# A transformer layer on one core: the compression MLP's first products in fp32 on four column quarters, instead of split in two and summed

## The chip, the cores and the metric

The kernel runs on one core of a Trainium2 chip. The metric is the device time of one execution in microseconds (us); the median of the runs is compared. Five engines work side by side, each through a queue of its own in program order: TensorE (PE, with its weight loads shown apart as PEld), VectorE (DVE), ScalarE (ACT), GpSimd (POOL) and SyncE (SP), which only issues transfers here. They meet at semaphores.

## The reference, cut to what matters

One layer of a causal decoder over 256 tokens of width 1024, in float32: RMSNorm, one input projection `h @ w_in` of 5656 columns, two attention mixers with a gated merge, `w_out`, and a gated convolutional MLP of width 2816. The change is in one small piece of the first mixer, the compression of its keys and values (two groups of 64 features each). Blocks of 32 tokens, 16 apart, are flattened and go through a small MLP; it is called once for keys and once for values:

```python
def compress(kv, pe, w1, w2):                    # kv: (1, 256, 2, 64), w1: (2048, 128)
    b16 = kv.reshape(B, S // 16, 16, G, dh)
    blocks = jnp.concatenate([b16[:, :-1], b16[:, 1:]], axis=2)      # 15 blocks of 32 tokens
    blocks = blocks + pe[None, None, :, None, :]
    flat = blocks.transpose(0, 1, 3, 2, 4).reshape(B, nc, G, 32 * dh)
    return jax.nn.gelu(flat @ w1) @ w2           # flat @ w1: contraction over 2048
```

`flat @ w1` is the piece: for each of the two calls 32 columns (2 groups x 16 places, of which 15 are used), a contraction over 2048 = 16 tiles of 128, and 128 outputs.

## The kernel before, in words

**Units.** All weights come as one stream of 128 x 2048 blocks, one block a unit, in a list `units` that one loop walks. A unit `u` is loaded by SP into a tile `u.raw` (pool `wraw`, three buffers of tag `raw`), split into two fp32r tiles by `hi_of` (ACT copies `raw` to `u.hi`, L127) and `lo_of` (DVE subtracts, `u.lo = raw - hi`, L131), multiplied on PE by `u.mm`, and the result in PSUM is written out by `u.evac`. Activations are split the same way (`hTh`, `hTl`), so that a product in full precision is three fp32r products: hi x hi and lo x hi (L180), hi x lo (L185), 48 matmuls of 256 moving columns for a usual unit. The tiles `hi` and `lo` have three buffers each too.

**Order.** The order on every engine is the order of the code in the loop; there is no scheduler. In step `i` of the loop: `load_to(i + 5)` issues loads up to unit `i + 4`; then the small work of attention; `lo_of(i + 1)`; `u.mm(u)` for unit `i`; `hi_of(i + 2)`; and `u.evac`. SP waits with a load until the buffer of `raw` that it goes to has been read.

**The stretch around the change.** Units 0 and 1 are multiplied first and together; unit 0 gives the raw keys and values for compression. `ev_cmp` scales them, adds the position term and writes a tile `f` of 128 x 4 x 256 (keys: parts 0 and 1, values: parts 2 and 3; a part has 32 columns `c` by 8 tiles `m`, with `m` running fastest). Unit 2 is a wider one. Units 3 and 4 are queries (`qa`). Units 5, 7 and 9 are queries of the second mixer (`qb`, evacuated on DVE by `ev_qb`, L448). **Units 6 and 8 are the weights `w1` of the compression**, for keys and for values. From unit 10 on come keys, values and gates of the second mixer, and from step 9 on the attention items run between the units' products.

**The compression before.** `split_cmp` splits `f` into `XC`, in which hi and lo columns stand side by side (L331 on ACT, L332 on DVE); `w1_hi` and `w1_lo` split units 6 and 8 on ACT (L404) and DVE (L409), hi and lo side by side as well. `mm_w1` (L419) then needs 16 matmuls for each of the two: 64 stationary columns (hi and lo of the activations), 256 moving columns (hi and lo of the weights), which fill a 64 x 256 corner of PSUM (`ph`). `cmp_sum`, `cmp_fold` add the parts up: S2 is built by ACT (L732) and DVE (L733), its lower half zeroed by POOL, and two small matmuls with the 0/1 matrix `E2` fold it (L740). `gates_of` (L429, L430) and `q_parts` (`QS`, L441 on ACT and L442 on DVE) are unrelated work that stands in DVE's queue between.

## Time and profile before

| | before |
|---|---|
| time, median of 3 runs | 396.79 us (402.17, 396.23, 396.79) |
| the profiled execution: own time | 396.06 us |
| its span in the trace | 394.3 us |
| PE busy | 387.1 us (98%), 3404 instructions |
| DVE busy | 292.5 us (74%) |
| ACT busy | 224.7 us (57%) |
| POOL busy | 32.0 us (8%) |
| granted clock of TensorE in the span | 0.998 |

Own time and span differ by 1.8 us, which lie outside the trace. PE's busy time counts overlapping records once; a record's duration is longer than the distance to the next record, since matmuls are pipelined, so that the pace is read from starts. An fp32 matmul shows as two records, an fp32r matmul as one.

### The profile page before, as it was taken

The page shows a single profiled execution, that of the slowest core. Times are in us where ns is not written, and L with a number is a line of the kernel's source. Part 1 is how long each engine was busy: PE and PEld are TensorE (multiplying, and loading weights), DVE is VectorE, ACT ScalarE, POOL GpSimd, SP SyncE. Part 2 cuts the span into 40 slices and gives each one's busy share as a digit, 9 for nine tenths or more (in the row PEclk, how much of TensorE's full clock was granted, in tenths as well). Part 3 has the DMA queues.
Part 4 walks back from the last instruction along what each step waited for, and adds up shares of the span by engine and source line. Part 5 has one row for each costly group of instructions (what it writes and reads, how often), then busy time and mean ns, then how long its engine had stood idle before and what let it go on. Part 6 is the DMA issues. An engine that isn't in the chain of part 4 may idle for free.

```text
span 394.3 us, 8025 instructions
## 1 busy us (share of the span) xinstructions
PE 387.1 (98%) x3404; PEld 381.1 (97%) x3404; DVE 292.5 (74%) x486; ACT 224.7 (57%) x316; POOL 32.0 (8%) x62
## 2 busy tenths in 40 slices
PE   8999999999999999999999999999999999999993
PEld 7999999999999999999999999999999999999993
DVE  5989899994877776468887599676594774947764
ACT  5987755774974665654644766545265452653513
POOL 7110000001000000250333000000000000000001
PEclk9999999999999999999999999999999999999999
DMA  7966673345233345452538246662734727347102
GB/s 275 418 252 257 244 264 134 126 175 235 108 109 114 117 170 183 167 182 111 199 153 288 86 170 240 233 235 103 304 128 194 251 104 287 135 185 263 59 0 106
DMA packets 11555, 72.60 MB, mean 184 GB/s; under 512 B 1280, under 2 KB 1664, under 8 KB 3584
## 3 DMA queue, kind: packets, MB, share of 16 engines
q1 hardware_dynamic: 11088, 71.25, 48.7%
q10 hardware_dynamic: 432, 0.85, 0.6%
q8 instruction: 26, 0.43, 0.4%
q14 instruction: 9, 0.07, 0.0%
HBM read 71.05 MB, written 1.05 MB: 183 GB/s over the span
## 4 chain that ended last, share of the span: by engine, by line
PE 92%; ACT 2%; DVE 2%; DMA 2%; issue 0%; POOL 0%; SPq 0%; POOLq 0%; ACTq 0%
PE ps_d L180 26%; PE ps_d L185 13%; PE ps_o L180 13%; PE ps_s L624 8%; PE ps_t L624 7%; PE ps_o L185 6%; PE ps_d L284 3%; PE ps_d L346 2%; PE ps_t L180 2%; DMA first<-in_first_dram 2%; PE ps_o L904 1%; PE ps_o L540 1%; PE ps_t L891 1%; PE ps_o L1028 1%; PE ps_s L180 1%; PE ps_d L419 1%
## 5 line engine op out<-in xcount | busy, mean ns | idle before, releaser
L131 DVE TENSOR_TENSOR wlo<-raw,whi 128x2048 fp32r<-128x2048 f32 (+2 forms) x62 | 134.7, 2175 | 0.9 <-ACT whi L127 0.7
L127 ACT ACTIVATE whi<-raw 128x2048 fp32r<-128x2048 f32 (+2 forms) x62 | 115.1, 1858 | 31.2 <-DMA raw<-in_wts_dram 27.2
L180 PE MATMUL ps_d<-hTh,whi 128*128 128x256 f32 x384 | 90.2, 280 | 0.0
L180 PE MATMUL ps_d<-hTl,whi 128*128 128x256 f32 x384 | 89.2, 278 | 0.0
L180 PEld LDWEIGHTS ps_d<-hTh,whi 128*128 128x128 f32 x384 | 72.2, 188 | 0.7 <-issue 0.5
L180 PEld LDWEIGHTS ps_d<-hTl,whi 128*128 128x128 f32 x384 | 72.3, 188 | 0.0
L185 PE MATMUL ps_d<-hTh,wlo 128*128 128x256 f32 x384 | 48.0, 278 | 0.0
L185 PEld LDWEIGHTS ps_d<-hTh,wlo 128*128 128x128 f32 x384 | 45.7, 188 | 0.1
L180 PE MATMUL ps_o<-hTh,whi 128*128 128x256 f32 x160 | 36.9, 277 | 0.0
L180 PE MATMUL ps_o<-hTl,whi 128*128 128x256 f32 x160 | 36.8, 277 | 0.0
L579 ACT ACTIVATE C<-U,small 128x256 f32<-128x256 f32 x22 | 12.0, 594 | 43.3 <-DVE U L575 43.3
L180 PEld LDWEIGHTS ps_o<-hTl,whi 128*128 128x128 f32 x160 | 30.1, 188 | 0.0
L180 PEld LDWEIGHTS ps_o<-hTh,whi 128*128 128x128 f32 x160 | 30.0, 188 | 0.0
L583 DVE SCALAR_TENSOR_TENSOR C<-U,small,C 128x256 f32<-128x256 f32 x44 | 19.4, 482 | 7.5 <-ACT C L579 7.4
L575 DVE TENSOR_TENSOR U<-ps_d,R 128x512 f32<-128x512 f32 x6 | 4.1, 691 | 22.1 <-PE ps_d L185 18.3
L185 PE MATMUL ps_o<-hTh,wlo 128*128 128x256 f32 x160 | 19.8, 276 | 0.0
L185 PEld LDWEIGHTS ps_o<-hTh,wlo 128*128 128x128 f32 x160 | 18.9, 188 | 0.0
L868 ACT ACTIVATE E<-E,ast 128x256 f32<-128x256 f32 (+1 forms) x32 | 14.2, 451 | 8.0 <-DVE ast L863 7.9
L575 DVE TENSOR_TENSOR U<-ps_o,R 128x512 f32<-128x512 f32 x5 | 3.4, 689 | 16.7 <-PE ps_o L185 16.7
L1254 POOL TENSOR_TENSOR tiny<-cst,tiny 128x1 f32<-128x1 f32 x2 | 0.4, 190 | 168.8 <-ACT sq L1253 168.8
L131 POOL TENSOR_TENSOR wlo<-raw,whi 128x1024 fp32r<-128x1024 f32 x3 | 7.7, 2573 | 74.1 <-ACT whi L127 74.1
L624 PE MATMUL ps_s<-whi,al 128*128 128x256 f32 x88 | 12.1, 276 | 0.0
(287 smaller groups left out, 768.7 us busy)
## 6 DMA issues: line engine op xcount, KB each, us to landing
raw<-in_wts_dram SPq DMA_DIRECT2D x61, 1024.0 KB, 4.8
first<-in_first_dram SPq DMA_DIRECT2D x7, 384.0 KB, 7.1
raw<-in_wts_dram SPq DMA_DIRECT2D x2, 560.0 KB, 9.0
xn<-in_xn_dram SPq DMA_DIRECT2D x2, 512.0 KB, 9.0
xT<-in_xT_dram SPq DMA_DIRECT2D x1, 1024.0 KB, 6.8
gf<-in_g_final_dram ACTq DMA_DIRECT2D x1, 512.0 KB, 3.6
out_dram<-Y SPq DMA_DIRECT2D x1, 512.0 KB, 2.6
out_dram<-Y SPq DMA_DIRECT2D x1, 320.0 KB, 2.4
```

What stands on the lines that cost most here:

```text
L127: A.activation(u.hi[:, u.o + c0:u.o + c1], u.raw[:, c0:c1], AF.Copy)
L131: (eng or V).tensor_sub(u.lo[:, u.o + c0:u.o + c1], u.raw[:, c0:c1], u.hi.bitcast(F32)[:, u.o + c0:u.o + c1])
L180: T.matmul(po, l, r, start=start and bank not in banks, stop=False, skip_group_check=True)
L185: T.matmul(po, l, r, start=False, stop=stop and n == len(ks) - 1, skip_group_check=True)
L284: T.matmul(u.p[:, i], l[:, kt, i * 128:i * 128 + 128], r[:, kt], start=kt == 0 and i == 0 and q == 0, stop=kt == 7 and q == 2, skip_group_ ...
L346: T.matmul(u.p[:, i], l[:, kt, i * 128:i * 128 + 128], r[:, kt], start=kt == 0 and i == 0 and q == 0, stop=kt == 7 and q == 2, skip_group_ ...
L419: T.matmul(p[0:64, i].rearrange("p h c -> p (h c)"), x, w[:, m % 8], start=m == 0, stop=m == 15, skip_group_check=True)
L575: V.tensor_tensor(out=U[:, :, 2:], in0=u.p, in1=bc(rt["R2"], 2), op=OP.mult)
L579: A.activation(C[:, c], U[:, c, 2:], AF.Identity, scale=CW(2, t), bias=CB[:, t:t + 1])
L583: V.scalar_tensor_tensor(C[:, c], U[:, c, w:w + S], CW(w, t), C[:, c], op0=OP.mult, op1=OP.add)
L624: T.matmul(ffn["y"][t][ch][:, b:e] if own is None else own, x[:, kt, t * 128:t * 128 + 128], w[:, kt, ch * 512 + b:ch * 512 + e], start=st ...
L868: A.activation(self.E[:, i], self.E[:, i], AF.Exp, bias=mn[:, i:i + 1], scale=-1.0, accum_out=dn[:, i:i + 1])
```

## The change

The compression's first products are made in fp32, without hi and lo. `f` itself is the stationary operand (32 columns for the first eight tiles of the contraction, 31 for the others, which start one block later), read in steps of eight elements, and the raw weights are the moving operand (128 columns). The 16 tiles of the contraction are dealt out to four column quarters of the array: tile `m` writes PSUM partitions 32 (m mod 4) and up, so that four sums stand below each other. The products of keys and values stand together, at step 8; step 6 has no product of its own. `E2` now adds up the four quarters, S2 is one ACT copy of 128 x 256.

The weights of units 6 and 8 no longer go through `raw`: they are loaded in two halves each to tiles of their own, `w1k` (tag MA, free after the first units) and `w1v` (two of the three buffers of tag PT, free until the attention needs them), and neither is split. `f` moves to tag MB. `lo_of(7)` now stands in step 5, behind `hi_of(7)`, instead of in step 6.

```diff
--- before.py
+++ after.py
@@ -85,8 +85,8 @@
 
 
 class Unit:
-    def __init__(self, n, mm, evac=None, split=None, pre=None, o=0):
-        self.n, self.mm, self.evac, self.split, self.pre, self.o = n, mm, evac, split, pre, o
+    def __init__(self, n, mm, evac=None, load=None, pre=None, o=0):
+        self.n, self.mm, self.evac, self.load, self.pre, self.o = n, mm, evac, load, pre, o
         self.raw = self.hi = self.lo = None
 
 
@@ -136,8 +136,10 @@
 
     def hi_of(i):
         if 2 <= i < len(units):
+            if units[i].load is not None:
+                return
             split_tiles(units[i])
-            (units[i].split or (split_hi, split_lo))[0](units[i])
+            split_hi(units[i])
 
     def lo_of(i):
         if 2 <= i < len(units):
@@ -152,13 +154,17 @@
                 split_lo(units[i], 0, 1024)
                 split_lo(units[i], 1024, 2048)
                 return
-            (units[i].split or (split_hi, split_lo))[1](units[i])
-
-    def load_range(u, c0, c1, q=None):
-        (q or nc.sync).dma_start(u.raw[:, c0:c1], bass.AP(tensor=a["wts"].tensor, offset=a["wts"].offset + u.off + c0,
+            if units[i].load is None:
+                split_lo(units[i])
+
+    def load_range(u, c0, c1, q=None, dst=None):
+        (q or nc.sync).dma_start(u.raw[:, c0:c1] if dst is None else dst, bass.AP(tensor=a["wts"].tensor, offset=a["wts"].offset + u.off + c0,
                                                           ap=[[u.n, 128], [1, c1 - c0]]))
 
     def load_unit(u):
+        if u.load is not None:
+            load_w1(u.load)(u)
+            return
         u.raw = wraw.tile([128, UW], F32, name="raw", tag="raw")
         load_range(u, 0, u.n)
 
@@ -304,14 +310,10 @@
 
     xr = {}
 
-    def xc_tile():
-        xr["XC"] = att.tile([128, 4, 8, 65], F32R, name="XC", tag="MB")
-        V.memset(xr["XC"].bitcast(F32)[:, :, :, 64], 0.0)
-
     def ev_cmp(u):
         R = rt["R"]
         t = att.tile([128, 2, 2, 128], F32, name="E", tag="E", bufs=2)
-        f = att.tile([128, 4, 256], F32, name="PT", tag="PT", bufs=3)
+        f = att.tile([128, 4, 256], F32, name="XC", tag="MB")
         p = u.p.rearrange("p i (s two) -> p two i s", two=2)
         Rv = R.rearrange("p (s two) -> p two s", two=2)
         for g in range(2):
@@ -326,11 +328,6 @@
                                 in1=pv[:, hf, i, None, :].to_broadcast([128, 32, 8]), op=OP.add)
         xr["f"] = f
 
-    def split_cmp(i):
-        f, XC = xr["f"][:, 2 * i:2 * i + 2].rearrange("p a (c m) -> p a m c", m=8), xr["XC"][:, 2 * i:2 * i + 2]
-        A.activation(XC[:, :, :, 0:32], f, AF.Copy)
-        V.tensor_sub(XC[:, :, :, 32:64], f, XC.bitcast(F32)[:, :, :, 0:32])
-
     def mm_first(u):
 
         for v in range(2):
@@ -393,31 +390,27 @@
     units.append(Unit(2048, lambda u: None, ev_ka))
 
 
-    def w1_parts(u, i):
-        dst = (u.hi, u.lo)[i]
-        r = u.raw[:, i * 1024:i * 1024 + 1024].rearrange("p (m c) -> p m c", m=8)
-        return [x[:, :2048].rearrange("p (m h c) -> p m h c", m=8, h=2) for x in (dst, dst.bitcast(F32))] + [r]
-
-    def w1_hi(u):
+    def mm_w1(u):
+        p = rt["ph"] = pd([2, 128])
         for i in range(2):
-            d, _, r = w1_parts(u, i)
-            A.activation(d[:, :, 0], r, AF.Copy)
-
-    def w1_lo(u):
-        for i in range(2):
-            d, h, r = w1_parts(u, i)
-            V.tensor_sub(d[:, :, 1], r, h[:, :, 0])
-
-    def mm_w1(i):
-        def f(u):
-            if i == 0:
-                rt["ph"] = pd([2, 2, 128])
-            p = rt["ph"]
             for m in range(16):
-                w = (u.hi, u.lo)[m // 8][:, :2048].rearrange("p (m c) -> p m c", m=8)
-                x = xr["XC"][:, 2 * i + m // 8, m % 8, m // 8:m // 8 + 64]
-                T.matmul(p[0:64, i].rearrange("p h c -> p (h c)"), x, w[:, m % 8], start=m == 0, stop=m == 15,
+                j, h = m % 4, m // 8
+                x = xr["f"][:, 2 * i + h].rearrange("p (c m) -> p m c", m=8)[:, m % 8, h:32]
+                T.matmul(p[32 * j:32 * j + 32 - h, i], x, xr["w1"][i][m // 8][:, m % 8], start=m < 4, stop=m > 11,
                          skip_group_check=True)
+
+    def load_w1(i):
+        if i == 0:
+            w = att.tile([128, 2, 8, 128], F32, name="w1k", tag="MA")
+            w = [w[:, h] for h in range(2)]
+        else:
+            w = [att.tile([128, 8, 128], F32, name="w1v", tag="PT", bufs=3) for _ in range(2)]
+
+        def f(u):
+            for h in range(2):
+                u.raw = w[h].rearrange("p m c -> p (m c)")
+                load_range(u, 1024 * h, 1024 * h + 1024, dst=u.raw)
+        xr.setdefault("w1", []).append(w)
         return f
 
     def ev_v(u):
@@ -453,7 +446,7 @@
         units.append(Unit(2048, lambda u: mm_plain(u, "t"), ev_k(qa, 2 * i, scale=-0.125)))
     for i in range(3):
         if i:
-            units.append(Unit(2048, mm_w1(i - 1), split=(w1_hi, w1_lo)))
+            units.append(Unit(2048, mm_w1 if i == 2 else lambda u: None, load=i - 1))
         units.append(Unit(2048, mm_plain, ev_qb(2 * i)))
     for i in range(3):
         units.append(Unit(2048, mm_plain, ev_k("kb", 2 * i)))
@@ -727,10 +720,7 @@
     def cmp_sum():
 
         S2 = att.tile([128, 2, 128], F32, name="S2", tag="c1")
-        P.memset(S2[64:128], 0.0)
-        p, s = rt["ph"][0:64], S2[0:64]
-        A.activation(s, p[:, :, 0], AF.Copy)
-        V.tensor_tensor(out=s, in0=p[:, :, 1], in1=s, op=OP.add)
+        A.activation(S2, rt["ph"], AF.Copy)
         cmp_["S2"] = S2
 
     def cmp_fold():
@@ -1083,8 +1073,7 @@
         for up, (g, s) in enumerate(pair):
             P.memset(scB[up * 64:up * 64 + 64, i:i + 1], -0.125 / SLOPE_B[s])
     E2 = att.tile([128, 32], F32, name="E2")
-    P.memset(E2[64:128], 0.0)
-    V.tensor_tensor(out=E2[0:64], in0=ident[0:64, 0:32], in1=ident[0:64, 32:64], op=OP.add)
+    V.tensor_reduce(out=E2, in_=ident.rearrange("p (j c) -> p c j", j=4), op=OP.add, axis=mybir.AxisListType.X)
     tabs["E2"] = E2
     tables_pool1()
     tables_pool2()
@@ -1145,7 +1134,7 @@
         for it in at(i):
             if isinstance(it, Dil):
                 it.split()
-        if i > 2:
+        if i > 2 and i != 6:
             lo_of(i + 1)
         if i == 10:
             cmp_gelu()
@@ -1156,9 +1145,6 @@
         if i == 3:
             hi_of(5)
             mixer_tiles()
-            xc_tile()
-            split_cmp(0)
-            split_cmp(1)
             u1.evac(u1)
         if i == 4:
             split_keys()
@@ -1189,6 +1175,8 @@
                 split_hi(units[3], c, c + 1024)
         if not 24 <= i <= 26 and i > 1 and i != 3:
             hi_of(i + 2)
+        if i == 5:
+            lo_of(7)
         if i == 2:
             u0.evac(u0)
             lo_of(3)
```

On PE, the rows from the last products of unit 5 to the first of unit 7, before (`whi` and `wlo` are a unit's hi and lo tiles, `ps_d` a PSUM bank). The same two L419 rows stand a second time, behind unit 7:

```order
L185 MATMUL ps_d<-hTh,wlo 128x256 x16
L419 MATMUL ps_d<-whi,XC 64x256 x8
L419 MATMUL ps_d<-wlo,XC 64x256 x8
L180 MATMUL ps_d<-hTh,whi 128x256
L180 MATMUL ps_d<-hTl,whi 128x256
```

After the change, the rows from the last products of unit 7 to the first of unit 9 (line numbers are those of the changed file: L191 was L185, L186 was L180, L399 is the new product):

```order
L191 MATMUL ps_d<-hTh,wlo 128x256 x16
L399 MATMUL ps_d<-w1k,XC 32x128 x8
L399 MATMUL ps_d<-w1k,XC 31x128 x8
L399 MATMUL ps_d<-w1v,XC 32x128 x8
L399 MATMUL ps_d<-w1v,XC 31x128 x8
L186 MATMUL ps_d<-hTh,whi 128x256
L186 MATMUL ps_d<-hTl,whi 128x256
```

Two runs of 16 fp32r matmuls have become one run of 32 fp32 matmuls between units 7 and 9; behind unit 5 nothing stands any more.

On DVE, from the evacuation of unit 5 to the lo tile of unit 10, before (`qb` is an evacuation of unit 5 or 7, `QS` and `gates` belong to attention, the 128x8x128 rows are the split of the compression's weights, L131 the lo tiles of units 7, 9 and 10, `S_748` is S2):

```order
L448 SCALAR_TENSOR_TENSOR qb<-ps_d,scB,R 128x256 x2
L131 TENSOR_TENSOR wlo<-raw,whi 128x2048
L442 SCALAR_TENSOR_TENSOR QS<-qa,QS 64x256 x4
L409 TENSOR_TENSOR whi<-raw,whi 128x8x128
L409 TENSOR_TENSOR wlo<-raw,wlo 128x8x128
L448 SCALAR_TENSOR_TENSOR qb<-ps_d,scB,R 128x256 x2
L442 SCALAR_TENSOR_TENSOR QS<-qa,QS 64x256 x4
L429 TENSOR_SCALAR gates<-gates 128x48
L430 RECIPROCAL gates<-gates 128x48
L131 TENSOR_TENSOR wlo<-raw,whi 128x2048
L733 TENSOR_TENSOR S_748<-ps_d,S_748 64x256
L131 TENSOR_TENSOR wlo<-raw,whi 128x2048
```

And after, from the evacuation of unit 4 (`qa`) on:

```order
L360 SCALAR_TENSOR_TENSOR qa<-ps_t,R 128x512
L131 TENSOR_TENSOR wlo<-raw,whi 128x2048
L441 SCALAR_TENSOR_TENSOR qb<-ps_d,scB,R 128x256 x2
L435 SCALAR_TENSOR_TENSOR QS<-qa,QS 64x256 x4
L441 SCALAR_TENSOR_TENSOR qb<-ps_d,scB,R 128x256 x2
L435 SCALAR_TENSOR_TENSOR QS<-qa,QS 64x256 x4
L422 TENSOR_SCALAR gates<-gates 128x48
L423 RECIPROCAL gates<-gates 128x48
L131 TENSOR_TENSOR wlo<-raw,whi 128x2048 x2
L441 SCALAR_TENSOR_TENSOR qb<-ps_d,scB,R 128x256 x2
```

The split of unit 8's weights and S2's sum have gone; the lo tile of unit 7 has moved ahead of unit 5's evacuation; what stands between unit 7's evacuation and unit 9's lo tile (QS and the gates) is the same as before.

On SP, the loads from the small inputs on, before (`raw` with 1120 columns is unit 2, the 16 are units 3 to 18):

```order
L158 DMA raw<-in_wts_dram 128x1120
L1068 DMA xn<-in_xn_dram 128x1024 x2
L158 DMA raw<-in_wts_dram 128x1120
L1070 DMA small<-in_small_dram 128x328
L158 DMA raw<-in_wts_dram 128x2048 x16
```

And after:

```order
L1060 DMA small<-in_small_dram 128x328
L161 DMA raw<-in_wts_dram 128x2048 x3
L161 DMA w1k<-in_wts_dram 128x1024 x2
L161 DMA raw<-in_wts_dram 128x2048
L161 DMA w1v<-in_wts_dram 128x1024 x2
L161 DMA raw<-in_wts_dram 128x2048 x10
```

The compression's weights are loaded in halves, in their old places in the queue, but to tiles that are free; so they, and the load behind them, wait for other things than before: `raw`'s three buffers now go round without units 6 and 8.

More of the change, by code (lines that the diff above doesn't have):

```diff
@@ L393, in build @@
     units.append(Unit(2048, lambda u: None, ev_ka))
-    def w1_parts(u, i):
-        dst = (u.hi, u.lo)[i]
-        r = u.raw[:, i * 1024:i * 1024 + 1024].rearrange("p (m c) -> p m c", m=8)
-        return [x[:, :2048].rearrange("p (m h c) -> p m h c", m=8, h=2) for x in (dst, dst.bitcast(F32))] + [r]
-    def w1_hi(u):
-        for i in range(2):
-            d, _, r = w1_parts(u, i)
-            A.activation(d[:, :, 0], r, AF.Copy)
-    def w1_lo(u):
-        for i in range(2):
-            d, h, r = w1_parts(u, i)
-            V.tensor_sub(d[:, :, 1], r, h[:, :, 0])
-    def mm_w1(i):
-        def f(u):
-            if i == 0:
-                rt["ph"] = pd([2, 2, 128])
-            p = rt["ph"]
-            for m in range(16):
-                w = (u.hi, u.lo)[m // 8][:, :2048].rearrange("p (m c) -> p m c", m=8)
-                x = xr["XC"][:, 2 * i + m // 8, m % 8, m // 8:m // 8 + 64]
-                T.matmul(p[0:64, i].rearrange("p h c -> p (h c)"), x, w[:, m % 8], start=m == 0, stop=m == 15,
-                         skip_group_check=True)
+    def mm_w1(u):
+        p = rt["ph"] = pd([2, 128])
+        for i in range(2):
+            for m in range(16):
+                j, h = m % 4, m // 8
+                x = xr["f"][:, 2 * i + h].rearrange("p (c m) -> p m c", m=8)[:, m % 8, h:32]
+                T.matmul(p[32 * j:32 * j + 32 - h, i], x, xr["w1"][i][m // 8][:, m % 8], start=m < 4, stop=m > 11,
+                         skip_group_check=True)
+    def load_w1(i):
[4 more added lines that the diff above has]
+            w = [att.tile([128, 8, 128], F32, name="w1v", tag="PT", bufs=3) for _ in range(2)]
+        def f(u):
+            for h in range(2):
+                u.raw = w[h].rearrange("p m c -> p (m c)")
+                load_range(u, 1024 * h, 1024 * h + 1024, dst=u.raw)
+        xr.setdefault("w1", []).append(w)
         return f
```

## The prediction, on record before the changed kernel ran

> **What bounds the kernel now.** First the page's head and the granted clock, then the engine that is busy nearly all the time:
>
> ```profile
> span 394.3 us, 8025 instructions
> PE 387.1 (98%) x3404; PEld 381.1 (97%) x3404; DVE 292.5 (74%) x486; ACT 224.7 (57%) x316; POOL 32.0 (8%) x62
> PE 92%; ACT 2%; DVE 2%; DMA 2%; issue 0%; POOL 0%; SPq 0%; POOLq 0%; ACTq 0%
> ```
>
> PE is busy for 98% and makes up 92% of the chain that ended last. A time saved on PE is therefore saved at the end, as long as no other engine holds PE afterwards. Whether one does at the place of the change is read from the stretches:
>
> ```profile
> core 0: us, PE busy (x) PEld busy (x) DVE busy (x) ACT busy (x) POOL busy (x), PEclk, DMA share, GB/s
> 40.00:48.00 8.00, 8.00 (x71) 8.00 (x69) 7.25 (x10) 6.58 (x12) 0.00 (x0) 1.00 0.72 265
> 48.00:56.00 8.00, 8.00 (x68) 7.74 (x65) 7.87 (x13) 4.10 (x3) 0.00 (x0) 1.00 0.58 198
> ```
>
> From 40 to 48 us, the stage of units 5 to 8, PE has no idle time at all, at full clock (1.00). From 48 to 56 us DVE is as full as PE (7.87 of 8.00 us): there DVE is near to holding PE. That place comes back below.
>
> **What goes.** The two old runs of the compression's products on PE, in order of time, with the products around them:
>
> ```profile
> 39.98 1.10 PE L419 MATMUL ps_d<-whi,XC 128*64 128x256 f32 x8
> ...
> 41.84 0.28 PE L180 MATMUL ps_d<-hTh,whi 128*128 128x256 f32 x1
> ...
> 47.50 1.10 PE L419 MATMUL ps_d<-whi,XC 128*64 128x256 f32 x8
> ...
> 49.37 0.28 PE L180 MATMUL ps_d<-hTh,whi 128*128 128x256 f32 x1
> ```
>
> The starts count, not the durations: the first run holds PE from 39.98 to 41.84, 1.86 us, the second from 47.50 to 49.37, 1.87 us; 16 matmuls at 0.117 us each. The first goes without a successor in its place: **-1.86 us**. The second is replaced.
>
> **What comes: 32 fp32 matmuls, four column quarters abreast.** Each shows as two records of 128 moving columns, 64 records. The trace has two relatives, the attention's fp32 products on column halves with the same 128 columns (L904), and one fp32 group on quarters with 256 columns (L780):
>
> ```profile
> 93.90 2.84 PE L904 MATMUL ps_o<-PT,Vn 128*64 128x128 f32 x48
> L904 PE MATMUL ps_o<-PT,Vn x96: 272/273/323, 93.9 to 121.5; 128*64 128x128 f32 x96
> ...
> 69.67 0.28 PE L851 MATMUL ps_s<-KL,QS 128*128 128x256 f32 x1
> 69.88 0.42 PE L780 MATMUL ps_o<-qa,kc 128*32 128x256 f32 x4
> ...
> 70.12 0.40 PE L780 MATMUL ps_o<-qa,kc 128*32 128x256 f32 x4
> ...
> L780 PEld LDWEIGHTS ps_o<-qa,kc x8: 106/108/109, 69.9 to 69.9; 128*32 128x32 f32 x8
> ```
>
> 48 records on halves take 2.84 us with the last one's 0.27 us, so 2.57 us from first to last start. They are 24 rounds of two, 23 steps: 0.112 us a round. On quarters, four records of 0.40 us begin within 0.42 - 0.40 = 0.02 us, and the next four 0.24 us after them: four do run abreast. A round on quarters with 128 columns is in no row; below it is bounded by half of the 0.24 us, 0.12, and by the halves' 0.112. I take 0.112, since that row has the same moving columns and the same kind of records. 64 records are 16 rounds: 15 x 0.112 + 0.02 = 1.70 us to the last start.
>
> Then the ends of the run. Into L780 the distance between starts is 69.88 - 69.67 = 0.21 instead of 0.117 (+0.09); the old run with 64 columns had no such step. Out of a column-tiled fp32 run back to the usual products:
>
> ```profile
> 144.82 1.04 PE L1028 MATMUL ps_o<-PT,vb 128*64 128x128 f32 x16
> 145.80 0.39 PE L180 MATMUL ps_d<-hTh,whi 128*128 128x256 f32 x1
> 146.02 0.28 PE L180 MATMUL ps_d<-hTl,whi 128*128 128x256 f32 x1
> ```
>
> With the median duration of 0.27 the last L1028 starts at 145.59; 0.21 us to the first product, 0.22 to the second, instead of 0.117 each: 0.21 is in the run, +0.10 behind it. The new run costs 1.70 + 0.21 + 0.09 + 0.10 = 2.10 us against 1.87: **+0.23 us**. The ends' price lies between nothing (the old run) and twice these rows (0.6 us).
>
> **A wait of before that goes.** Where PE and DVE were equally full, this stands:
>
> ```profile
> 52.90 0.28 PE L180 MATMUL ps_d<-hTl,whi 128*128 128x256 f32 x1
> 53.06 0.50 PE L185 MATMUL ps_d<-hTh,wlo 128*128 128x256 f32 x2
> ...
> 47.70 0.88 DVE L448 SCALAR_TENSOR_TENSOR qb<-ps_d,scB,R 128x256 f32<-128x256 f32 x2 [0.48 <-PE ps_d L185]
> 48.61 1.55 DVE L442 SCALAR_TENSOR_TENSOR QS<-qa,QS 64x256 fp32r<-64x256 f32 x4
> 50.41 0.45 DVE L430 RECIPROCAL gates<-gates 128x48 f32<-128x48 f32 x1
> 50.78 2.23 DVE L131 TENSOR_TENSOR wlo<-raw,whi 128x2048 fp32r<-128x2048 f32 x1
> ```
>
> Unit 9's lo products start at 53.06, 0.16 us after the product before them, just when its lo tile is done on DVE (50.78 + 2.23 = 53.01), and the second is 0.22 us behind the first (0.50 - 0.28): 0.05 + 0.11 us lost. DVE's chain to that tile begins when unit 7's products end (DVE waits for them until 47.70), and the same four pieces stand in it after the change. So the lo tile comes at a fixed distance, 53.01 - 47.70 = 5.31 us, behind unit 7, while PE now arrives 0.23 us later than before: the wait is over by then, **-0.16 us**. It also sets a floor: had the new run been shorter than the old one, PE would wait here and nothing more would be won than 1.86.
>
> **Off PE.** What the other engines lose, one row for each kind:
>
> ```profile
> L332 DVE TENSOR_TENSOR XC<-PT,XC x2: 1129/1142/1156, 29.2 to 30.3; 128x512 fp32r<-128x512 f32 x2
> L409 DVE TENSOR_TENSOR whi<-raw,whi x2: 1218/1222/1226, 36.9 to 44.9; 128x1024 fp32r<-128x1024 f32 x2
> 52.92 0.40 DVE L733 TENSOR_TENSOR S<-ps_d,S 64x256 f32<-64x256 f32 x1
> L404 ACT ACTIVATE whi<-raw x2: 1061/1062/1062, 34.8 to 39.7; 128x1024 fp32r<-128x1024 f32 x2
> L331 ACT ACTIVATE XC<-PT x2: 1205/1206/1206, 27.9 to 29.0; 128x512 fp32r<-128x512 f32 x2
> ```
>
> DVE loses 2 x 1.14 + 4 x 1.22 + 0.40 = 7.6 us, ACT 4 x 1.06 + 2 x 1.21 = 6.7. I cost all of it at nothing: PE had no idle time in these stretches, and the one chain that holds PE contains none of these pieces, since DVE sat idle for 0.48 us ahead of it. S2 becomes one ACT copy right behind the run; its reader L740 stands behind unit 9's 48 products. `E2`'s reduction runs on DVE at the start, while the first inputs are on their way. `lo_of(7)` now waits for ACT's `hi_of(7)`, and unit 5's evacuation is queued behind it on DVE, so I follow unit 7:
>
> ```profile
> 20.45 19.11 SPq L158 DMA_DIRECT2D raw<-in_wts_dram  x5
> 24.27 4.48 DVE L131 TENSOR_TENSOR wlo<-raw,whi 128x2048 fp32r<-128x2048 f32 x2
> 32.14 1.29 ACT L384 ACTIVATE KH<-E 64x512 fp32r<-64x512 f32 x2 [1.90 <-DVE E L381]
> 36.24 0.69 DVE L363 SCALAR_TENSOR_TENSOR qa<-ps_t,R 128x512 f32<-128x512 f32 x1
> DMA to landing us min/median/max: 4.6/4.8/11.8
> ```
>
> SP issued five loads between 20.45 and 39.56; now it issues seven blocks in that time, since two no longer wait for `raw`. Unit 7's block waits for unit 3's lo tile, the first of the two in the second row, 26.5 us, and lands by 31.3 at the median. ACT comes to it behind four KH copies of 0.65 us, which begin no later than at 32.14: done by 36.7. PE needs it at 39.98. By the slowest landing, 11.8, the copy of 1.9 us would end at 40.2, 0.3 late. `lo_of(7)`, behind `qa` and as long as half of the second row, ends at 36.9 + 2.2 = 39.1, before unit 5 does on PE. `w1v`, issued behind unit 7's block, lands between 32 and 39 by the same rows; its products start near 45.6. Units 9 to 11 are loaded earlier than before. So nothing is late next; if that cover went, I put the price at up to 2 us, one hi copy.
>
> **The sum**, against the profiled execution's own time of 396.06 (span 394.3, 1.8 outside it): -1.86 + 0.23 - 0.16 = -1.79, which gives **394.3 us**. The median of the three runs shown, 396.79, lies 0.7 above that execution, the fastest (396.23) 0.2; I expect the changed kernel's median between 394.3 and 395.0 and say **394.6 us**, 0.5% less. A measurement of this kernel can hardly tell less than 2%, 7.9 us, from no change, so this is "within 2%".
>
> **The strided operand.** The stationary operand is now read in steps of eight fp32, 32 bytes. ScalarE read the same tile in the same steps in L331, 1206 ns for 512 elements; here is as much in order, and the weight loads by their width:
>
> ```profile
> L384 ACT ACTIVATE KH<-E x2: 629/631/633, 32.1 to 32.8; 64x512 fp32r<-64x512 f32 x2
> L419 PEld LDWEIGHTS ps_d<-whi,XC x16: 133/134/138, 39.9 to 48.2; 128*64 128x64 f32 x16
> L180 PEld LDWEIGHTS ps_d<-hTh,whi 128*128 128x128 f32 x384 | 72.2, 188 | 0.7 <-issue 0.5
> ```
>
> 1206 against 631 ns is 1.9 times. The Trainium skill, "SBUF — State Buffer", section "Door 1: The DMA port swizzle", says that SBUF delivers lines of 16 bytes and that each access that goes to a new line pays; by it each of the 32 columns would pay, and the two ACT rows agree in kind. What steps cost a weight load no row shows. Loads of 32, 64 and 128 columns take 108, 134 and 188 ns, some 27 for each 32 columns; 1.9 times that is 51, which hides under a round of 112 if the four quarters load side by side. L780's eight loads all begin at 69.9, in less than 8 x 27, so I take them as side by side and the price as 0.
>
> **The rivals.**
>
> *Strided loads set the pace (0.06).* Through one port a round would be 4 x 51 = 204 ns, 16 rounds 3.3 us, +1.5: 395.8. For it stands ACT's factor of 1.9, against it how close L780's loads begin.
>
> *The issue sets the pace (0.10).* If PE could not take up records faster than the 2.57 / 47 = 55 ns that L904 shows, 64 would take 3.5 us, +1.8: 396.1. For it: no row shows more than eight records faster than that. Against it: those eight of L780, 0.26 us from the first start to the last. The Trainium skill, "TensorE: Matmul & The Clock Gate", section "Wait — 56ns, not 53.3ns?", gives some 62 ns of sequencer time for a matmul with hardware decode off; by it 64 would be 4.0 us and the whole 396.5. L904's 55 ns lie below it, so a single record does not pay it; a matmul of two records may.
>
> *The quarters do not overlap (0.06): slower.* Place: the run between units 7 and 9. Price: a record then costs what fp32 records of 128 columns cost that follow each other on the whole array:
>
> ```profile
> 70.45 1.09 PE L891 MATMUL ps_t<-ident,E 128*128 128x128 f32 x8
> ```
>
> (1.09 - 0.28) / 7 = 0.116 us. 64 of them are 7.4 us, +5.7: 400.0, 1% slower. It turns at a pace of 55 ns a record, where the 1.79 us are used up (1.79 / 64 = 28 on top of 27). Against it stand L780's four abreast; for it, that L780 has only two rounds.
>
> *A block comes late (0.05).* The earlier loads collide, unit 7's or `w1v`'s wait reaches PE: up to 2 us, 394.6 to 396.6. The change then does on PE what it says and gives it back in a wait; the slowest landing speaks for it, the slack of 3 us at the median against.
>
> *More is won (0.05).* DVE's 7.6 freed microseconds take away waits that I have not seen, another 1 us: 393.5. Against it, the list of waits has a single row for PE, the one for the very first matmul:
>
> ```profile
> PE ps_t L1074 <- DVE kc L1076: 1.0, 1, 1.0
> ```
>
> **Chances and range.** My forecast has 0.68 with 394.0 to 395.4 (its ends: the run's ends at nothing or at twice the price, and the 0.7 between execution and median). The rivals reach from 393.5 to 400.0; leaving the serial case out, 393.7 to 396.7 holds some 8 in 10. Only something that no row shows is over 2% away: faster 0.01, same 0.97, slower 0.02.
>
> **What would show it.** The new run's 64 records begin within 1.7 us; the first unit-7 product follows unit 5's last by 0.12 us; unit 9's lo products follow without the 0.16; DVE falls by some 7 us and ACT by 6 without any effect on the span. A step between rounds of over 0.112, a PE wait ahead of unit 7, or a wait of the run for `w1v` would make it wrong.

## The result and the profile after

The changed kernel took 393.01 us against 396.23 (medians of five runs each): a ratio of 0.9919, 95% interval 0.9893 to 0.9945. That is within 2% of no change, as said, but below the range that the prediction gave (393.7 to 396.7). One run of each was some 2% longer (402.17 and 400.92); the ratios here and below leave such runs out and so need not be those of the two medians beside them. Its profiled execution took 392.86, with a span of 391.0. In the page of the changed kernel the rows that answer to those of before:

```profile
span 391.0 us, 8068 instructions
PE 383.8 (98%) x3436; PEld 377.7 (97%) x3436; DVE 285.6 (73%) x478; ACT 218.5 (56%) x310; POOL 32.4 (8%) x60
PE 93%; ACT 2%; DVE 2%; DMA 1%; issue 0%; POOL 0%; POOLq 0%; ACTq 0%
```

PE is still busy for 98%, and still makes 93% of the chain. DVE lost 6.9 us and ACT 6.2, about as forecast. Now the places of the change, from the timeline of PE (start, time from the first start to the last end of the group, then engine, line and tiles; L186 and L191 are before's L180 and L185, L399 is the new `mm_w1`):

```profile
39.15 0.84 PE L191 MATMUL ps_d<-hTh,wlo 128*128 128x256 f32 x6
39.83 0.28 PE L186 MATMUL ps_d<-hTh,whi 128*128 128x256 f32 x1
...
44.70 0.73 PE L191 MATMUL ps_d<-hTh,wlo 128*128 128x256 f32 x5
45.36 1.11 PE L399 MATMUL ps_d<-w1k,XC 128*32 128x128 f32 x32
46.29 1.06 PE L399 MATMUL ps_d<-w1v,XC 128*32 128x128 f32 x32
47.27 0.38 PE L186 MATMUL ps_d<-hTh,whi 128*128 128x256 f32 x1
47.49 0.28 PE L186 MATMUL ps_d<-hTl,whi 128*128 128x256 f32 x1
```

Unit 5's last product starts at 39.15 + 0.84 - 0.28 = 39.71 and unit 7's first at 39.83: 0.12 apart, the first run is gone. The new run goes from 45.36 to 47.27, 1.91 us, which is the forecast's 1.70 + 0.21 to the hundredth. It begins 0.21 behind unit 7's last product (44.70 + 0.73 - 0.28 = 45.15), and the second product behind it follows by 0.22: both ends cost what the neighbours' rows had said. Behind it, PE and DVE at unit 9's lo products:

```profile
50.91 0.28 PE L186 MATMUL ps_d<-hTl,whi 128*128 128x256 f32 x1
51.02 0.73 PE L191 MATMUL ps_d<-hTh,wlo 128*128 128x256 f32 x5
```

```profile
45.47 0.88 DVE L441 SCALAR_TENSOR_TENSOR qb<-ps_d,scB,R 128x256 f32<-128x256 f32 x2 [3.00 <-PE ps_d L191]
...
48.55 4.42 DVE L131 TENSOR_TENSOR wlo<-raw,whi 128x2048 fp32r<-128x2048 f32 x2
```

The lo products follow by 0.11, without a wait. DVE's chain begins at 45.47; its lo tile, the first half of the group of two, is done at about 48.55 + 2.2 = 50.76, 5.29 behind, and PE comes at 51.02. The floor of the prediction, PE arriving ahead of this tile, is 0.26 us away.

So all that was forecast happened where it was forecast. Yet the two profiled executions differ by 3.20 us, not by 1.79. The rest lies in products that the change does not touch. Sixteen lo products of one unit, before (L185) and after (L191), for units 10, 11, 14 and 28:

```profile
60.00 1.98 PE L185 MATMUL ps_d<-hTh,wlo 128*128 128x256 f32 x16
66.96 2.05 PE L185 MATMUL ps_d<-hTh,wlo 128*128 128x256 f32 x16
90.11 2.05 PE L185 MATMUL ps_d<-wlo,hTh 128*128 128x256 f32 x16
192.19 2.05 PE L185 MATMUL ps_o<-mixh,wlo 128*128 128x256 f32 x16
```

```profile
57.97 2.05 PE L191 MATMUL ps_d<-hTh,wlo 128*128 128x256 f32 x16
64.86 1.98 PE L191 MATMUL ps_d<-hTh,wlo 128*128 128x256 f32 x16
87.78 1.98 PE L191 MATMUL ps_d<-wlo,hTh 128*128 128x256 f32 x16
189.68 1.98 PE L191 MATMUL ps_o<-mixh,wlo 128*128 128x256 f32 x16
```

In these rows sixteen products take either 1.98 us or 2.05: (1.98 - 0.28) / 15 = 0.113 us from start to start, or 0.118. Across the trace the steps of these products nearly all average 113.3 or 117.8 ns over six in succession, at a granted clock of 1.00 in both, with no wait in between. A pace mostly holds for a unit of 48 products (0.21 us a unit), sometimes for many units. The changed kernel has the quick pace at unit 7, 11, 14 and from unit 28 to the first up-projections (the stretch from 187 to 213 us in before), and the slow one at unit 10.

### The profile page after: what moved, and what is told of

It reads as the page before. It is cut to its first block, busy times and chain, and to the rows that moved or that the text cites. A ratio compares the mean times of both kernels' runs of the same rounds, so it can differ in the third digit from the quotient of the medians.

```text
span 391.0 us, 8068 instructions
## 1 busy us (share of the span) xinstructions
PE 383.8 (98%) x3436; PEld 377.7 (97%) x3436; DVE 285.6 (73%) x478; ACT 218.5 (56%) x310; POOL 32.4 (8%) x60
## 4 chain that ended last, share of the span: by engine, by line
PE 93%; ACT 2%; DVE 2%; DMA 1%; issue 0%; POOL 0%; POOLq 0%; ACTq 0%
PE ps_d L186 26%; PE ps_d L191 13%; PE ps_o L186 13%; PE ps_s L617 8%; PE ps_t L617 7%; PE ps_o L191 6%; PE ps_d L343 3%; PE ps_d L290 3%; PE ps_t L186 2%; PE ps_o L894 1%; PE ps_o L533 1%; PE ps_t L881 1%; PE ps_o L1018 1%; PE ps_s L186 1%; PE ps_t L191 1%; PE ps_t L993 1%
## 5 line engine op out<-in xcount | busy, mean ns | idle before, releaser
L131 DVE TENSOR_TENSOR wlo<-raw,whi 128x2048 fp32r<-128x2048 f32 (+2 forms) x62 | 134.6, 2175 | 0.8 <-ACT whi L127 0.7
L186 PE MATMUL ps_d<-hTh,whi 128*128 128x256 f32 x384 | 90.1, 280 | 0.0
L186 PE MATMUL ps_d<-hTl,whi 128*128 128x256 f32 x384 | 89.0, 277 | 0.0
L186 PEld LDWEIGHTS ps_d<-hTh,whi 128*128 128x128 f32 x384 | 72.2, 188 | 0.9 <-issue 0.7
L186 PEld LDWEIGHTS ps_d<-hTl,whi 128*128 128x128 f32 x384 | 72.2, 188 | 0.0
L191 PE MATMUL ps_d<-hTh,wlo 128*128 128x256 f32 x384 | 47.8, 277 | 0.0
L191 PEld LDWEIGHTS ps_d<-hTh,wlo 128*128 128x128 f32 x384 | 45.6, 188 | 0.0
L186 PE MATMUL ps_o<-hTh,whi 128*128 128x256 f32 x160 | 36.9, 277 | 0.0
L186 PE MATMUL ps_o<-hTl,whi 128*128 128x256 f32 x160 | 36.8, 276 | 0.0
L186 PEld LDWEIGHTS ps_o<-hTh,whi 128*128 128x128 f32 x160 | 30.0, 188 | 0.0
L186 PEld LDWEIGHTS ps_o<-hTl,whi 128*128 128x128 f32 x160 | 30.0, 188 | 0.0
L191 PE MATMUL ps_o<-hTh,wlo 128*128 128x256 f32 x160 | 19.8, 276 | 0.0
L191 PEld LDWEIGHTS ps_o<-hTh,wlo 128*128 128x128 f32 x160 | 18.9, 188 | 0.0
L131 POOL TENSOR_TENSOR wlo<-raw,whi 128x1024 fp32r<-128x1024 f32 x3 | 7.7, 2570 | 74.1 <-ACT whi L127 74.1
```

The lines of the kernel that those rows point to most:

```text
L131: (eng or V).tensor_sub(u.lo[:, u.o + c0:u.o + c1], u.raw[:, c0:c1], u.hi.bitcast(F32)[:, u.o + c0:u.o + c1])
L186: T.matmul(po, l, r, start=start and bank not in banks, stop=False, skip_group_check=True)
L191: T.matmul(po, l, r, start=False, stop=stop and n == len(ks) - 1, skip_group_check=True)
```

## The experiments

Three theories of the pace stood ahead of them. **Theory 1, the lock**: there are two steady paces; a break in the stream of products (another shape, a wait) sets which of them follows, and it stays until the next break. **Theory 2, traffic**: the slow pace is that of stretches with more transfers or more work of other engines beside PE. **Theory 3, placement**: it is decided by where the change has put its tiles. By 2 or 3 the extra 1.4 us are an effect of the change.

### The same two kernels again

No edit; before:

> The kernel before once more, unchanged, to see which stretches of the usual products stand at which pace. In the first profile they stood at 117.8 ns from product to product in unit 7, unit 11, unit 14 and from 187 to 213 us (units 27 to 32), and at 113.3 ns in most others. Theory 1 (a lock): PE has two steady paces, 113.3 and 117.8; the last disturbance ahead of a stretch (a wait, a change of tiling, an fp32 group) sets which one, by its exact timing. Then the pattern may differ from one execution to the next in some stretches, always by these two values. Theory 2 (traffic): the work of the other engines slows PE; the program is the same, so the same stretches stand at 117.8. Theory 3 (placement of tiles): the same stretches, exactly.

The changed kernel:

> The changed kernel once more, unchanged. In its first profile unit 7 and units 27 to 32 stood at 113.3 ns. Theory 1: unit 7 is at 113.3 again, since nothing disturbs PE between units 5 and 7 now; units 27 to 32 may be at either pace, and the span then moves by up to 1.2 us. Theories 2 and 3: the same pattern as in the first profile.

Measured: 395.04 and 391.31 (before's median in that comparison: 394.79). The pattern of before is another one: units 3 to 5, quick in its first profile, are slow, unit 7 is quick, and from unit 28 on it is quick. In the changed kernel units 21 to 23 were slow at first and are quick now. The view by source line shows the pace of units 28 to 30 by the duration of one product (min/median/max); the first row is before's first profile, the second its second:

```profile
L185 PE MATMUL ps_o<-mixh,wlo x48: 281/282/282, 192.2 to 205.3; 128*128 128x256 f32 x48
```

```profile
L185 PE MATMUL ps_o<-mixh,wlo x48: 276/276/276, 191.4 to 204.0; 128*128 128x256 f32 x48
```

The same program with the same placement ran the same stretch at both paces: **theory 3 falls**, and so does theory 2, as far as traffic is what the program orders.

### Before, with more breaks

The kernel before has a `kick`, one extra product of 64 columns ahead of a unit's own, at unit 24 and once in the MLP. Here four more units get one:

```diff
-        if i in (24, NFIRST + 2):
+        if i in (7, 11, 14, 24, 28, NFIRST + 2):
```

> The kernel before, with one more small product (64 moving columns, its result is overwritten) ahead of units 7, 11, 14 and 28, as the code has it already ahead of two others. Theory 1: the disturbance sets the pace anew, so that some of these units, above all 28 to 32, run at 113.3 instead of 117.8: up to 0.2 us less a unit, 0.9 for 28 to 32, less 0.1 to 0.2 for each kick; in all 0.5 to 1.0 us faster. Theories 2 and 3: the pace stays at 117.8 in these units, and the kernel is 0.4 to 0.8 us slower.

Measured: 395.68 against 394.79, ratio 1.0015 (1.0001 to 1.0030). Theory 1 had expected 0.5 to 1.0 us less; the time is that which theories 2 and 3 expected, but not the paces: units 11 and 14 came out quick, unit 28 and the units behind it slow, kick or not. Units 11 and 28:

```profile
66.50 1.98 PE L185 MATMUL ps_d<-hTh,wlo 128*128 128x256 f32 x16
...
191.64 2.05 PE L185 MATMUL ps_o<-mixh,wlo 128*128 128x256 f32 x16
```

A break can change the pace, as theory 1 says, but does not choose it: the gain that I had hoped for in a tuned set of kicks is not there.

### The changed kernel, with the old splits left on DVE and ACT

To see whether "off PE at nothing" holds: the compression's weights are still split at the old places, into tiles that nothing reads, and `lo_of(7)` goes back to step 6. PE's work is that of the changed kernel.

```diff
+                for h, w in enumerate(xr["w1"][units[i].load]):
+                    A.activation(w1_half(units[i], h)[0][:, :, 0], w, AF.Copy)
...
+            for h, w in enumerate(xr["w1"][units[i].load]):
+                d, d32 = w1_half(units[i], h)
+                V.tensor_sub(d[:, :, 1], w, d32[:, :, 0])
```

> The changed kernel, with the splits of the compression's weights left in on ACT (4 x 1.06 us) and DVE (4 x 1.22 us), at their old places and into tiles of the hi and lo rings as before; their results are not used, and the lo tile of unit 7 is back in step 6. My reckoning put their removal at nothing: then the span is that of the changed kernel within 0.5 us, except for stretches whose pace is set otherwise (theory 1). Theory 2: the extra gain of 1.5 us over my sum came from the relief of ACT and DVE, and goes again: units 27 to 32 are far behind these splits and would not change, units 7 to 11 would stand at 117.8. Theory 3: the rings' places shift, so the pattern of the two paces changes.

Measured: 394.21, ratio to before 0.9985 (0.9973 to 0.9997): most of the gain is gone. PE's and DVE's timelines of this kernel (its lines are shifted: L196 and L201 are the usual products, L451 is `ev_qb`, L164 the split that was left in):

```profile
47.70 0.36 PE L196 MATMUL ps_d<-hTh,whi 128*128 128x256 f32 x1 [0.66 <-DVE qb L451]
...
52.04 0.73 PE L201 MATMUL ps_d<-hTh,wlo 128*128 128x256 f32 x4 [0.33 <-DVE wlo L131]
```

```profile
45.55 1.22 DVE L164 TENSOR_TENSOR wlo<-w1v,wlo 128x1024 fp32r<-128x1024 f32 x1
46.69 0.87 DVE L451 SCALAR_TENSOR_TENSOR qb<-ps_d,scB,R 128x256 f32<-128x256 f32 x2
```

PE, 1.87 us ahead of before, waits 0.66 us for the evacuation of `qb`, which stands in DVE's queue behind a split, and 0.33 us for unit 9's lo tile. So DVE's relief, with `lo_of(7)` moved forward, gives PE nothing by itself, but it is what lets PE keep the first run's 1.87 us: without it 1.0 us of them turn into new waits. The prediction priced the relief at nothing: right as a gain of its own, wrong as a condition of the others.

### The changed kernel over more runs, with its quarters apart, in another order, and without the steps

First once more as it is:

> The changed kernel, word for word, over more runs. The sum of the places that the change touches is -1.79 us (0.9955); what the first comparison showed beyond it, another 1.4 us, lay in the pace of the usual products, 113.3 or 117.8 ns. Theory 1 (the pace is set at a disturbance and kept): the mean over many runs lies between 0.990 and 0.996, the pace of each stretch is again one of the two values, with units 7, 11 and 14 at 113.3 and unit 10 at 117.8 as in both profiles of the changed kernel, and units 27 to 32 at either. Rival (the relief of DVE takes waits away): no stretch differs from the first profile of the changed kernel, and the ratio is 0.992 again.

Measured: 392.56 against 394.84, ratio 0.9933 (0.9915 to 0.9951). The pattern is that of the first profile again, with the quick pace from unit 28 on.

**Two runs instead of one**: keys at step 6, values at step 8.

```diff
-        for i in range(2):
+        for i in (u.load,):
...
-            units.append(Unit(2048, mm_w1 if i == 2 else lambda u: None, load=i - 1))
+            units.append(Unit(2048, mm_w1, load=i - 1))
```

> The quarters' products in two runs, the keys' right behind unit 5 where the old kernel had its first run, the values' behind unit 7. By the first profile of the changed kernel a run of eight rounds holds PE for 0.206 in, 0.02 + 0.165 + 6 x 0.109 to its last start, 0.202 out and 0.11 behind it: 1.36 us, against 0.11 to the next product where there is no run, so +1.14 for the first run; the second is shorter than the one joint run by 8 x 0.109 = 0.87. If nothing but PE counted that is +0.27 against the changed kernel: 0.9928 + 0.0007. If the floor of the prediction holds (unit 9's lo tile comes 5.31 us behind unit 7's end on DVE), PE, which reaches it 0.87 us earlier after unit 7, waits there: +1.1 us against the changed kernel, 0.995 to 0.996 against before, with a wait of 0.5 to 0.9 us ahead of unit 9's first lo product.

Measured: 394.25, ratio 0.9976 (0.9961 to 0.9990). In this kernel L401 is `mm_w1` and L443 `ev_qb`; first PE, then DVE:

```profile
39.98 1.11 PE L401 MATMUL ps_d<-w1k,XC 128*32 128x128 f32 x32
41.11 0.35 PE L186 MATMUL ps_d<-hTh,whi 128*128 128x256 f32 x1
...
51.79 0.28 PE L186 MATMUL ps_d<-hTl,whi 128*128 128x256 f32 x1
52.40 0.86 PE L191 MATMUL ps_d<-hTh,wlo 128*128 128x256 f32 x5 [0.33 <-DVE wlo L131]
```

```profile
47.04 0.88 DVE L443 SCALAR_TENSOR_TENSOR qb<-ps_d,scB,R 128x256 f32<-128x256 f32 x2 [4.51 <-PE ps_d L191]
```

Each run takes 1.13 us to the product behind it, more than half of the joint run's 1.91. Most of the 0.78 us that the shorter second run gives is lost at the floor: unit 9's lo products start 0.61 us behind the product ahead of them (51.79) instead of 0.11, when DVE's lo tile is there, 5.36 behind the start of DVE's chain (47.04). The median is 1.7 us over the changed kernel's; 1.1 were expected, and 1.08 are found when the pace is taken out (the table below).

**Another order** of the 16 tiles: the four of one quarter follow each other.

```diff
-            for m in range(16):
+            for m in sorted(range(16), key=lambda m: m % 4):
```

> The same 32 matmuls in another order: the four k tiles of one quarter follow each other, instead of going round the four quarters. If it is the overlap of neighbouring records on different quarters that makes the run 1.71 us long, a record now follows the one before it on its quarter by 0.107 to 0.116 us and the run takes 64 x 0.11 = 7 us, +5.0 to +5.7: 398 us, 1.0045 to 1.007 against before. If the queues of the four quarters run apart from each other, the order makes no difference: 1.71 us and the time of the changed kernel.

Measured: 395.03, ratio 0.9997 (0.9982 to 1.0013). Neither expectation holds: the run takes 4.51 us.

```profile
44.48 2.26 PE L399 MATMUL ps_d<-w1k,XC 128*32 128x128 f32 x29
46.48 0.33 PE L399 MATMUL ps_d<-w1v,XC 128*32 128x128 f32 x1
46.58 0.27 PE L399 MATMUL ps_d<-w1k,XC 128*31 128x128 f32 x1
46.64 0.27 PE L399 MATMUL ps_d<-w1v,XC 128*32 128x128 f32 x1
46.69 0.27 PE L399 MATMUL ps_d<-w1k,XC 128*31 128x128 f32 x1
...
46.86 2.20 PE L399 MATMUL ps_d<-w1v,XC 128*32 128x128 f32 x29
48.99 0.39 PE L186 MATMUL ps_d<-hTh,whi 128*128 128x256 f32 x1
```

The values' first record (46.48, on the first quarter) starts ahead of records of the keys that were issued before it (46.58 to 46.80, on the last quarter), and from there the two quarters alternate. Records on one quarter follow by 0.11 us, and most of the time two quarters are at work: the order costs 2.6 us (4.51 - 1.91), half of the 5.0 to 5.7 that one quarter at a time would have cost. So the overlap makes the run short, and the order round the quarters is what gets four of them abreast. The Trainium skill, "TensorE: Matmul & The Clock Gate", section "The mechanism", says that matmuls keep program order in start and end. The rows above differ, and on column quarters the measurement decides.

**Without the steps**: `f` is kept with the 32 columns of a stationary operand side by side, and DVE writes it in steps instead.

```diff
-        fv = f.rearrange("p (i h) (c m) -> p h i c m", h=2, m=8)
+        fv = f.rearrange("p (i h) (m c) -> p h i c m", h=2, m=8)
```

> The channel sums are kept with the 32 columns of one stationary operand side by side in memory; VectorE writes them in steps instead. If the steps of 32 bytes cost the weight loads nothing that shows (the prediction), the run stays at 64 records within 1.71 us, rounds of 0.109. If the loads in steps set the pace of a round, rounds become shorter than 0.109.

Measured: 393.85 in one run. The weight loads and records of the keys' products, in the changed kernel and in this one:

```profile
L399 PEld LDWEIGHTS ps_d<-w1k,XC x32: 134/137/162, 45.4 to 46.1; 128*32 128x32 f32 x16, 128*31 128x31 f32 x16
L399 PE MATMUL ps_d<-w1k,XC x32: 272/273/328, 45.4 to 46.2; 128*32 128x128 f32 x16, 128*31 128x128 f32 x16
```

```profile
L399 PEld LDWEIGHTS ps_d<-w1k,XC x32: 106/109/110, 45.0 to 45.7; 128*32 128x32 f32 x16, 128*31 128x31 f32 x16
L399 PE MATMUL ps_d<-w1k,XC x32: 272/273/297, 45.0 to 45.8; 128*32 128x128 f32 x16, 128*31 128x128 f32 x16
```

Reading in steps costs 137 - 109 = 28 ns a load, about the 24 ns (51 - 27) that the prediction had estimated, and it is hidden, as the prediction said: the records keep their 273 ns, and the run takes 1.88 us instead of 1.91 (44.96 to 46.84), 0.03 at its first round.

### More profiles, and what is left when the pace is taken out

Before, a third and a fourth time, and the changed kernel a fourth:

> The kernel before once more, for a third profile of its pattern. The times that the stretches at the pace of 117.8 ns cost above 113.3, summed over the run of the usual products, were 2.75 and 2.20 us in its first two profiles; from unit 1's first product to PE's last matmul, less that sum, it took 368.21 and 368.30 us. If that sum and the landing of the first inputs are all that differs between executions (the lock), this profile has 368.2 to 368.4 again, whatever its pattern. If the times between stretches vary too, it leaves that band.

> As the third: 368.2 to 368.4 us from unit 1's first product to the end, less the slow pace's sum. On units 27 to 32 the two earlier profiles of before disagree (117.8 and 113.3): these two tell which is the more usual; if the slow pace there belongs to the kernel before and the fast one to the changed kernel, both are at 117.8.

> The changed kernel once more. The three earlier profiles had 366.23, 366.60 and 366.56 us from unit 1's first product to the end, less a slow pace's sum of 1.56, 0.57 and 1.18 us; the lock expects 366.2 to 366.6 and units 27 to 32 at either pace, a pattern that belongs to the kernel expects 113.3 there.

And breaks in the changed kernel, where its first profile was slow:

```diff
-        if i in (24, NFIRST + 2):
+        if i in (10, 17, 21, 22, 23, 24, NFIRST + 2):
```

> The changed kernel with one extra product of 64 columns (the kernel's own kick) ahead of units 10, 17, 21, 22 and 23, which ran at 117.8 ns in its first profile. A kick took 0.13 us in the kernel before (four of them 0.5 us) and freed two units of two that were slow in the first half, 0.22 us each; it did not free units 28 to 32. If a kick draws the pace anew and mostly gives 113.3, the sum is 5 x 0.13 - 5 x 0.22 = -0.45 us against the changed kernel, 0.992 against before; if the pace comes from something else, +0.65, 0.995.

Measured: 395.45 and 394.64 for before, 392.23 for the changed kernel; 394.88 with the kicks, 1.0004 (0.9992 to 1.0016) against before's 394.62, slower than either expectation (0.992 and 0.995). The kicked kernel's lo products at units 10, 11, 14 and 28:

```profile
57.18 1.98 PE L191 MATMUL ps_d<-hTh,wlo 128*128 128x256 f32 x16
64.14 2.05 PE L191 MATMUL ps_d<-hTh,wlo 128*128 128x256 f32 x16
87.48 2.05 PE L191 MATMUL ps_d<-wlo,hTh 128*128 128x256 f32 x16
190.43 2.05 PE L191 MATMUL ps_o<-mixh,wlo 128*128 128x256 f32 x16
```

The kick at unit 10 made unit 10 quick and units 11 and 14 slow, which had no kick: at these three units that is the pattern of before. The kick at 17 made that unit quick, those at 21 to 23 freed one of the three, and everything from unit 24 to 212 us is slow. This single profile points to a pace that depends on what came ahead, several units back; the extra breaks had no lasting good.

For every profile the table gives **A**, the time from unit 2's first product (the expectations call it unit 1's) to the start of PE's last matmul; **S**, what the slow pace adds (each step between products of 256 columns where six in succession average 117.3 to 118.2 ns, less 113.3); and the rest. The expectations above had counted S a little otherwise, with steps of other products and of the time before unit 2 in it; here all profiles are counted alike.

| profile | unit 7 | 10 | 11, 14 | 21-23 | from 28 | A | S | A - S |
|---|---|---|---|---|---|---|---|---|
| before, first | slow | quick | slow | slow | slow | 370.96 | 2.54 | **368.42** |
| before, second (also 3-5 slow) | quick | quick | slow | slow | quick | 370.50 | 1.99 | **368.51** |
| before, third | slow | quick | slow | slow | quick | 370.01 | 1.59 | **368.42** |
| before, fourth | slow | quick | slow | slow | quick | 370.01 | 1.56 | **368.45** |
| before, four kicks | quick | quick | quick | slow | slow | 370.70 | 1.79 | 368.91 |
| changed, first | quick | slow | quick | slow | quick | 367.79 | 1.14 | **366.65** |
| changed, second | quick | slow | quick | quick | quick | 367.17 | 0.53 | **366.64** |
| changed, timed again | quick | slow | quick | slow | quick | 367.74 | 1.14 | **366.60** |
| changed, fourth | quick | slow | quick | slow | quick | 367.78 | 1.17 | **366.61** |
| without steps | quick | quick | slow | slow | slow | 369.30 | 2.66 | 366.64 |
| splits left in | quick | slow | quick | slow | slow | 370.16 | 2.27 | 367.89 |
| quarters apart | slow | slow | quick | slow | quick | 369.22 | 1.51 | 367.71 |
| other order | quick | slow | quick | slow | quick | 370.35 | 1.14 | 369.20 |
| changed, five kicks | quick | quick | slow | mixed | slow | 370.15 | 2.92 | 367.22 |

Without the pace, four profiles of before agree within 0.09 us and four of the changed kernel within 0.05. Between their means lie 368.45 - 366.63 = **1.82 us**; the prediction's sum was 1.79. The other rows are that plus their own price: the splits left in 1.26, of which 0.99 stand as waits, the quarters apart 1.08 (1.1 were expected), the other order 2.57, a kick 0.12.

## Why the prediction was wrong, and where it was right

**Right, place by place.** The first run went for 1.87 us (1.86 forecast). The run of quarters takes 1.91 with its way out, its ends cost 0.09 and 0.10, the wait ahead of unit 9's lo products is gone. Of the rivals, the steps do not set the pace (28 ns a load, hidden); the issue does not (four records of a round start within 0.02 us, and 32 matmuls in the 1.71 us from first to last start are 53 ns each); the quarters do overlap, and the price of that rival was too high for a mere change of order (2.6 measured, 5.7 named); no block came late, since PE's only listed wait is the one of before. "Off PE at nothing" holds as the change was made, but only because the splits go with the products; the floor at unit 9, named there, is real, and without the relief 1.26 us of the gain are lost. The Trainium skill, "TensorE: Matmul & The Clock Gate", section "Wait — 56ns, not 53.3ns?", gives some 62 ns for each matmul with hardware decode off; at 53 ns each this run did not pay that.

**Wrong: the step from the sum to the time.** The prediction says that the sum is made against the profiled execution's own 396.06, and that the median lies between 394.3 and 395.0. In this it took the rest of PE's work for fixed: neither the sum nor the range has a term for the pace of the products that the change does not touch. It was not fixed: S was 2.54 us in that execution and is 1.14 in the changed kernel's, 1.40 less. Between these two executions A falls by 370.96 - 367.79 = 3.17 us: 1.77 in A - S, as forecast, and 1.40 in S. Their whole times differ by 3.20. The 1.40 have two parts:

- 0.98 us from unit 28 on. Before was slow there in one profile of four, the changed kernel in none of four, variants of either in four of six. The execution from which I started is the unusual one among the profiles in this, and its 396.06 about 1 us too high as a base; before's median in the three later comparisons was 394.6 to 394.8. It was not that execution alone: four of before's five runs in the first comparison lay at 395.56 to 396.79. They were not profiled, so whether the same stretch was slow in them is open. That the change makes the quick pace likelier there is not shown either.
- 0.42 us at units 7, 10, 11 and 14: unit 7 slow in three of four profiles of before and in none of the changed kernel; 11 and 14 slow in all four, then in none; 10 the other way round. This comes again in each profile (at unit 7 in all but one), so I count it to the change: with the new stream ahead of them these units run at another pace. Why is not shown, and it hangs on little: the one profile without the steps, whose run is 0.03 us shorter, has 11 and 14 slow and 10 quick again. With the 0.42 the change is worth 1.82 + 0.42 = 2.24 us on an execution that is quick from unit 28 on, 0.57%: a ratio of 0.9943, which both intervals hold (0.9893 to 0.9945, 0.9915 to 0.9951). The medians of the longer comparison differ by 394.84 - 392.56 = 2.28.

The rival "more is won" (393.5, chance 0.05) had the sign and nearly the size, but another mechanism, waits that DVE's relief takes away. The list of PE's waits was right against it. What I did not look at were the steps between starts of products that wait for nothing: the trace of before already showed 1.98 and 2.05 us for the same sixteen products, and my terms were made with 0.117 without asking why 0.113 stood elsewhere.

## What to carry to other kernels

Before a prediction is set on a base, look whether like instructions run at like steps everywhere; where they run at two, work out what part of the base is the slow one, and give that part a range of its own, because it can come out otherwise in the next execution, or with an edit ahead of it. An effect of a fraction of a per cent is best read from the trace at the places that the edit touches, and a second profile of the same program tells what the rest does by itself. When work leaves an engine that is almost as full as the bottleneck, ask whether the bottleneck's gain needs that relief: here over half of it became waits without that (0.99 of 1.82 us).

## What was not expected of the hardware

- Products of 256 moving columns, 128 rows by 128, run at 113.3 or at 117.8 ns a step, with durations of 276 or 281 ns, at a granted clock of 1.00. Extra breaks in the stream changed the pace of some units and not of others; a pace held from one unit of 48 products to some 400 (five kicks, 164 to 212 us). What decides it stays open; the program's order, the transfers that it asks for and the place of its tiles do not fix it, since the same program showed both.
- Column quarters do not keep program order among each other: a record on one quarter starts ahead of records on another that were issued before it (46.48 against 46.58 to 46.80 us). With the four tiles of a quarter in succession, mostly two quarters were at work at a time (4.51 us for 64 records); round the quarters, four (1.91).
- Loading 32 stationary columns in steps of 32 bytes takes 137 ns, side by side 109; beside records of 273 ns it cost 0.03 us in all.
